# Attention's preparation rebuilt: norm scale folded into the weights' split, rows turned tile by tile, wide rotary tables; unused products during the second router's rounds

## The chip, the cores and the metric

One core of a Trainium2 chip runs one program. Its five engines each work through their own list of instructions: TensorE (PE, with its weight loads shown apart as PEld), VectorE (DVE), ScalarE (ACT), GpSimd (POOL) and SyncE (SP), which here only starts transfers. They wait for each other through semaphores. The metric is the device time of one execution in microseconds. Times inside the program are counted from the start of the profiled span.

## The reference

Two layers over 512 tokens of width 1024. Each layer mixes tokens (layer 0 by gated long convolutions, layer 1 by attention), adds a cross attention into 256 memory tokens, and then runs a mixture of 16 experts in which each expert picks its 64 best tokens. The lines that matter here:

```python
def rms_norm(x, g):
    y = xf * lax.rsqrt(jnp.mean(xf * xf, axis=-1, keepdims=True) + NORM_EPS)
    return (y * g.astype(jnp.float32)).astype(x.dtype)
...
mem_n = rms_norm(mem, mem_norm_g)
for i in range(DEPTH):
    u = rms_norm(h, mix_norm_g[i])
    if i % N_MIXERS == 0:
        proj = u @ hy_w_in[j]
        ...
    else:
        proj = u @ at_w_in[j]          # 1024 -> 768 q, 256 k, 256 v, 256 for the cross attention
        q = apply_axial_rope(rms_norm(q, at_q_norm_g[j]), cos, sin)
        kk = apply_axial_rope(rms_norm(kk, at_k_norm_g[j]), cos, sin)
        main = blocked_gqa(q, kk, vv)
    cross = memory_cross_attn(cq, mem_n, w_mem_kv[i])
    h = h + jnp.concatenate([main, cross], axis=-1) @ w_out[i]
    h = h + expert_choice_ffn(rms_norm(h, ffn_norm_g[i]), router_w[i], ...)

def expert_choice_ffn(xn, w_router, w_gate, w_up, w_down):
    aff = jax.nn.softmax((xn @ w_router).astype(jnp.float32), axis=-1)
    g, idx = lax.top_k(jnp.swapaxes(aff, 1, 2), cap)      # cap = 64
    xg = xn[bidx, idx]
    hid = silu(xg @ w_gate) * (xg @ w_up)
    y = (hid @ w_down) * g
    return jnp.zeros_like(xn).at[bidx, idx].add(y)
```

## The kernel before

By the trace the program passes through these stretches: layer 0's mixing up to about 378 us, its router up to 415, its experts up to 755, attention with its preparation up to 1016, the second router up to 1033, the second layer's experts up to 1381, and the last norm.

The residual `h` stays in SBUF as four tiles of 128 tokens by 1024. Products that need more than fp32r's precision are made of three: a number is split into a rounded high part and the rest, and `mm3` (lines 283 to 285) adds high by high, low by high and high by low. `split` (lines 230 to 240) makes the parts: ACT rounds the high one (L234 without a scale, L236 with one) and DVE, or POOL when asked, subtracts it to give the low one (L238 without, L240 with a scale). `Pair` holds both parts. `put` calls `split` on slices of a `Pair`.

A router (in `moe`, from line 937) turns the affinities onto 16 partitions by four transposes (L966), finds the 64 largest per expert in eight rounds of MAX8 and MATCH_REPLACE8 on DVE (L989, L990), turns the result back (L1000, into the bank `wb`), counts ranks (L1004, L1007), builds the one-hot matrix `oh`, and gathers the chosen rows with products (L1040) and their row factors (L1021). In layer 0 the memory's key and value products for layer 1 (`mem_kv`, L331 and L335) are issued behind the first transposes, so that PE has work beside the rounds. In layer 1 nothing stands there.

The experts' weights come through a ring of slots of 768 KB, all started by SP in one order (L524). A slot is loaded anew once the PE products that used it have run, and the first of these are the gate products L1071. The last pair's rows are added to `h` by scatter products (L1094 and L1095, pinned, that is kept in program order) and adds on DVE (L1096), eight of each; ACT takes the squares of each half tile as it is done (L1158).

Attention then loads its input weights in four blocks of 384 columns (`load_at`). DVE multiplies each by the norm's gain first (L1179, eight slices of 128 by 384 a block), then `split_at` splits it, with the low parts made in turn by POOL and DVE. The rotary tables are made on POOL (L1209, L1210, L1212) in pieces of 128 by 32. All four tiles of `h` are turned by transposes (L1228) after all scatter products, in two halves `k4` of 512 columns. Blocks are projected in the order 2 (keys and half of the values), 0, 1, 3, each tile by tile into one of two banks tagged `p`. The bank is freed by `norm_rope` (L1244 squares on ACT, L1246 to L1251 on DVE, and then L1254, L1259 on POOL and L1261 for the rotation). `head_T` (L1295 copies, L1298 transposes) starts the heads, and L1321 and L1322 are the score products.

The order on each engine is set by a scheduler that models the instructions. Only what is pinned or issued after another instruction by name is kept fixed.

Of the kernel before, what the change touches and what calls it, by code (L numbers as in the profile page):

```python
# [17 lines left out]
T = 512  # L18
# [10 lines left out]
NE = 16  # L29
# [120 lines left out]
def kernel(  # L150
# [80 lines left out]
    def split(src, hi, lo, scale=None, eng=None):  # L231
# [705 lines left out]
    def moe(layer, rt, ring):  # L937
# [61 lines left out]
        for tt in range(NT):  # L999
            PE.transpose(out=wb[:, tt * NE:(tt + 1) * NE], in_=work[:, tt * 128:(tt + 1) * 128], identity=ident[:NE, :NE])  # L1000
# [90 lines left out]
        def scatter(y, ohT, tt, n, tag):  # L1091
            sl = slice(n * 512, (n + 1) * 512)
            b = bank(tag)
            pin(PE.matmul(b, ohT.ap[:, tt * 128:(tt + 1) * 128], y.hi, start=True, stop=False))  # L1094
            pin(PE.matmul(b, ohT.ap[:, tt * 128:(tt + 1) * 128], y.lo, start=False, stop=True))  # L1095
# [6 lines left out]
        for pr in range(NE // 2):  # L1102
# [33 lines left out]
            else:  # L1136

                sq, hss = xgb.ap[:, :512], small.tile([128, 2, NT], F32, name="hsq", bufs=1)
# [14 lines left out]
            if pr == last:  # L1153
                y1 = parts(1)
                for tt in range(NT):
# [12 lines left out]
    hss = moe(0, rt, ring)  # L1168
    if stop == "moe0":
        return dump()  # L1170


    def load_at(blk):
# [3 lines left out]
        wv = fv(wb, ND, 384)  # L1177
        for k in range(ND):
            DVE.tensor_scalar(out=wv[:, k], in0=wv[:, k], scalar1=vec(MIXG + 8 + k), scalar2=None, op0=ALU.mult)  # L1179
        return wb  # L1180

    def split_at(wb, first=False):
        W = Pair(RB, ND, 384)
        for k in range(ND):
            put(W, (ALLP, k), fv(wb, ND, 384)[:, k], eng=(POOL, DVE)[[0, 1, 0, 1, 0, 1, 0, 1][k]])
# [3 lines left out]
    wb = load_at(2)  # L1189
    atpool = tc.tile_pool(name="at", bufs=1, side="right")  # L1190
    for p in RX:
        p.turn(F32R)
# [316 lines left out]
```

## Time and profile before

| what | us |
|---|---|
| median of three runs | 1397.52 (1394.19 to 1398.58) |
| the profiled execution | 1396.28 |
| its span | 1394.3 |
| PE busy | 1278.1 (92%) |
| DVE, ACT, POOL busy | 628.8 (45%), 432.9 (31%), 208.0 (15%) |
| moved by DMA over the span | 364.06 MB, mean 261 GB/s |

Busy shares are averages over stretches with different limits, so the table says little about a single stretch. A stretch is read from the windows (busy time of each engine, PE's granted clock as a share of full speed, the share of the 16 DMA engines) and from the timeline, where a bracket behind a row gives the idle time ahead of it and what ended it. An fp32 product of the program shows as two matrix instructions in the trace, a transpose as one.

### The profile page before, as it was taken

What the parts mean: (1) busy time and instruction counts of PE and PEld (TensorE: products, weight loads), DVE (VectorE), ACT (ScalarE), POOL (GpSimd) and SP (SyncE); (2) the same over time, 40 slices, a digit from 0 to 9 for tenths busy, and PEclk for the clock granted to TensorE, in tenths of its full rate; (3) what the DMA queues carried; (4) which work ended last, traced back from release to release, by engine and by line L of the source; (5) the groups of instructions that cost most, each with busy time, mean ns of one, the idle gap of its engine ahead of it and who ended that gap; (6) DMA issues with size and microseconds to landing.
All of it is one profiled execution on the core that took longest, in us unless ns stands there. A gap on an engine that the chain in (4) does not pass through costs nothing.

```text
span 1394.3 us, 17952 instructions
## 1 busy us (share of the span) xinstructions
PE 1278.1 (92%) x6986; PEld 816.9 (59%) x6986; DVE 628.8 (45%) x1239; ACT 432.9 (31%) x844; POOL 208.0 (15%) x207
## 2 busy tenths in 40 slices
PE   7998999989989999999888789999959999998985
PEld 5887878865775444444434787656744444443432
DVE  5567757777451222221214778567541222221213
ACT  6444445545221011100003458685311110110003
POOL 4342334323200000000002432021100000000001
PEclk8999999999999999999999999999969999999998
DMA  9312101315898999999998001123869999999994
GB/s 349 114 31 61 48 29 46 122 46 179 272 359 344 416 416 417 416 417 417 416 407 356 1 0 62 46 86 105 303 263 371 417 417 416 416 416 417 417 416 197
DMA packets 79046, 364.06 MB, mean 261 GB/s; under 512 B 8497, under 2 KB 17073, under 8 KB 77682
## 3 DMA queue, kind: packets, MB, share of 16 engines
q1 hardware_dynamic: 73552, 343.96, 62.7%
q0 software_dynamic: 2592, 11.54, 2.2%
q10 hardware_dynamic: 2818, 7.43, 1.4%
q8 instruction: 55, 0.90, 0.3%
q14 instruction: 29, 0.24, 0.1%
HBM read 354.51 MB, written 8.39 MB: 260 GB/s over the span
## 4 chain that ended last, share of the span: by engine, by line
PE 57%; DMA 23%; DVE 12%; ACT 3%; issue 3%; POOL 2%; SPq 0%; DVEq 0%; ACTq 0%; POOLq 0%
PE bank_e L1071 8%; PE bank_p L1071 8%; DMA farena<-in_exp_w_gate_dram 6%; DMA x<-in_exp_w_down_dram 4%; DMA x<-in_exp_w_up_dram 4%; PE bank_p L284 4%; PE bank_p L283 4%; PE bank_p L285 4%; PE bank_y L1146 4%; PE bank_e L1146 3%; PE bank_y L1342 1%; DMA farena<-p_atw_dram 1%; PE bank_m L1040 1%; DMA farena<-p_hyw_dram 1%; DMA farena<-in_exp_w_up_dram 1%
## 5 line engine op out<-in xcount | busy, mean ns | idle before, releaser
L1096 DVE TENSOR_TENSOR h<-h,bank_m 128x512 f32<-128x512 f32 x64 | 41.4, 683 | 244.8 <-PE bank_m L1095 244.8
L284 PE MATMUL bank_p<-x,x 128*128 128x512 f32 (+1 forms) x284 | 111.0, 391 | 4.0 <-POOL x L238 3.4
L285 PE MATMUL bank_p<-x,x 128*128 128x512 f32 (+1 forms) x288 | 109.6, 380 | 0.2 <-DVE x L238 0.2
L1071 PE MATMUL bank_e<-x,farena 128*64 128x384 f32 x496 | 102.8, 489 | 5.3 <-DMA x<-in_exp_w_up_dram 5.3
L1071 PE MATMUL bank_p<-farena 128*64 128x384 f32 x480 | 97.9, 490 | 8.2 <-DMA farena<-in_exp_w_gate_dram 8.2
L1025 POOL DMA_INDIRECT rows<-h_keep,rows_at x14 | 13.3, 953 | 568.3 <-DVE rows_at L1024 537.8
L240 DVE SCALAR_TENSOR_TENSOR rarena<-bank_y,gs,rarena 128x512 fp32r<-128x512 f32 x16 | 12.0, 750 | 176.1 <-ACT rarena L236 176.1
L1071 PE MATMUL bank_e<-farena 128*64 128x384 f32 x408 | 86.1, 489 | 4.8 <-DMA farena<-in_exp_w_up_dram 4.8
L1071 PE MATMUL bank_p<-x,farena 128*64 128x384 f32 x416 | 84.3, 489 | 3.9 <-DMA x<-in_exp_w_gate_dram 3.9
L283 PE MATMUL bank_p<-x,x 128*128 128x512 f32 (+1 forms) x216 | 84.3, 391 | 2.2 <-DVE h L434 1.1
L1082 ACT COPY earena<-bank_m 128x384 f32<-128x384 f32 x32 | 15.3, 479 | 227.0 <-PE bank_m L1080 227.0
L234 ACT CAST x<-farena 128x1024 fp32r<-128x1024 f32 (+2 forms) x100 | 69.3, 717 | 50.2 <-DMA farena<-p_hyw_dram 14.7
L1120 ACT ACTIVATE earena<-bank_p,gs 128x384 f32<-128x384 f32 x32 | 18.6, 581 | 194.0 <-PE bank_p L1071 194.0
L238 POOL TENSOR_TENSOR x<-farena,x 128x384 fp32r<-128x384 f32 (+2 forms) x31 | 52.5, 1705 | 174.5 <-ACT x L234 162.5
L1071 PEld LDWEIGHTS bank_e<-x,farena 128*64 128x64 f32 x496 | 42.2, 137 | 51.8 <-issue 38.7
L1071 PEld LDWEIGHTS bank_p<-farena 128*64 128x64 f32 x480 | 39.6, 137 | 52.4 <-issue 36.5
L1146 PE MATMUL bank_e<-x,earena 128*64 128x512 f32 x174 | 62.0, 596 | 3.2 <-DMA x<-in_exp_w_down_dram 3.2
L284 PEld LDWEIGHTS bank_p<-x,x 128*128 128x128 f32 x284 | 54.5, 192 | 15.8 <-POOL x L238 5.6
L1146 PE MATMUL bank_y<-x,earena 128*64 128x512 f32 x168 | 61.7, 599 | 0.9 <-DMA x<-in_exp_w_down_dram 0.7
L434 DVE TENSOR_TENSOR h<-h,bank_p 128x512 f32<-128x512 f32 x64 | 43.7, 684 | 39.0 <-PE bank_p L285 38.7
L236 ACT ACTIVATE rarena<-bank_y,gs 128x512 fp32r<-128x512 f32 x16 | 11.0, 687 | 159.1 <-PE bank_y L1146 126.2
L285 PEld LDWEIGHTS bank_p<-x,x 128*128 128x128 f32 x288 | 55.7, 193 | 7.4 <-issue 0.8
(359 smaller groups left out, 2912.5 us busy)
## 6 DMA issues: line engine op xcount, KB each, us to landing
x<-in_exp_w_up_dram SPq DMA_DIRECT2D x62, 768.0 KB, 15.0
farena<-in_exp_w_gate_dram SPq DMA_DIRECT2D x60, 768.0 KB, 15.0
farena<-in_exp_w_down_dram SPq DMA_DIRECT2D x57, 768.0 KB, 15.0
x<-in_exp_w_down_dram SPq DMA_DIRECT2D x57, 768.0 KB, 15.0
x<-in_exp_w_gate_dram SPq DMA_DIRECT2D x52, 768.0 KB, 15.0
farena<-in_exp_w_up_dram SPq DMA_DIRECT2D x51, 768.0 KB, 14.4
slot<-in_exp_w_gate_dram SPq DMA_DIRECT2D x16, 768.0 KB, 15.0
slot<-in_exp_w_up_dram SPq DMA_DIRECT2D x15, 768.0 KB, 15.0
```

Of the source, the lines that this page charges most:

```text
L234: ACT.copy(out=hi.ap if isinstance(hi, Blk) else hi[0], in_=src)
L238: return (eng or DVE).tensor_tensor(out=lo[0], in0=src, in1=hi[1], op=ALU.subtract)
L283: PE.matmul(o, L.hi[li], R.hi[ri], start=first, stop=False)
L284: PE.matmul(o, L.hi[li], R.lo[ri], start=False, stop=False)
L285: PE.matmul(o, L.lo[li], R.hi[ri], start=False, stop=last)
L434: DVE.tensor_tensor(out=h[:, tt, sl], in0=h[:, tt, sl], in1=b, op=ALU.add)
L1040: pin(PE.matmul(b[:, j * 128:(j + 1) * 128], h[:, tt, 256 * q + j:256 * (q + 1):2], ohv[:, tt], start=tt == 0, stop=tt == NT - 1))
L1071: pin(PE.matmul(banks[n][64 * e:64 * e + 64, :384], xg[:, k, 64 * e:64 * e + 64], ring.at[(nm, 2 * pr + e, q)][0][:, j, n * 384:(n + 1) * ...
L1082: ACT.copy(out=hT[n].ap, in_=b[:, :384])
L1096: DVE.tensor_tensor(out=h[:, tt, sl], in0=h[:, tt, sl], in1=b, op=ALU.add)
L1120: ACT.activation(out=hid[n].ap, in_=gb[n][:, :384], func=AF.Silu, scale=rss)
L1146: pin(PE.matmul(yb[n][64 * e:64 * e + 64], hT[g].ap[:, k * 128 + 64 * e:k * 128 + 64 * e + 64], ring.at[("d", 2 * pr + e, g, c)][0][:, i % ...
```

## The change

Five edits, all in `moe` and in attention's preparation.

1. In layer 0's router the first of four chunks of `mem_kv` is issued ahead of the affinities' transposes and is no longer bound to come after them.
2. In layer 1's router a new helper `keep_warm` issues eleven fp32 products of the identity with itself, 512 columns wide, into a bank that nobody reads; the transposes into `wb` are kept behind them.
3. Layer 0's `moe` gets `attention_begin`, which is called per tile between the last scatter products. It loads and splits block 2's weights, and turns each tile's rows once that tile is complete. The second half of the columns is split by ACT and a product with the negated identity instead of by DVE. The squares come last, into a scratch of their own in another arena.
4. `load_at` no longer scales. `split_at` folds the gain into the split: ACT's high part by L236, DVE's low part by L240, none on POOL. The weights' parts and the turned rows now lie in the ring's pieces alone.
5. The rotary tables are made four token tiles at a time, 16 products and 4 negations in place of 32 and 8.

```diff
+    def keep_warm(n):
+        b = bank("p")
+        for _ in range(n):
+            tc.keep_in_program_order(PE.matmul(b, ident, ident.unsqueeze(1).broadcast_to([128, 4, 128]), start=True, stop=True))
...
-    def moe(layer, rt, ring):
+    def moe(layer, rt, ring, then=None):
...
         if layer == 0:
+            kv = mem_kv(mTb, lambda c: mws[c], xr.rearrange("p (a b) -> p a b", a=4))
+            next(kv)
             with tc.issue_after(turned.ins):
-                drain(mem_kv(mTb, lambda c: mws[c], xr.rearrange("p (a b) -> p a b", a=4)))
+                drain(kv)
...
+        else:
+            keep_warm(11)
...
-            PE.transpose(out=wb[:, tt * NE:(tt + 1) * NE], in_=work[:, tt * 128:(tt + 1) * 128], identity=ident[:NE, :NE])
+            t = PE.transpose(out=wb[:, tt * NE:(tt + 1) * NE], in_=work[:, tt * 128:(tt + 1) * 128], identity=ident[:NE, :NE])
+            if layer:
+                tc.keep_in_program_order(t)
...
                 for tt in range(NT):
                     for n in range(2):
-                        scatter((y0, y1)[n], ohT[pr], tt, n, "me"[n])
-                        ACT.activation(out=sq, in_=h[:, tt, n * 512:(n + 1) * 512], func=AF.Square, accum_out=hss[:, n, tt:tt + 1])
+                        scatter((y0, y1)[n], ohT[pr], tt, n, "me"[n], (lambda ins: ins) if then else pin)
+                        if not then:
+                            squares(tt, n)
+                    if then and tt:
+                        then(tt - 1)
+                if then:
+                    then(NT - 1)
+                    for tt in range(NT):
+                        for n in range(2):
+                            squares(tt, n, pin)
...
-        for k in range(ND):
-            DVE.tensor_scalar(out=wv[:, k], in0=wv[:, k], scalar1=vec(MIXG + 8 + k), scalar2=None, op0=ALU.mult)
...
-            put(W, (ALLP, k), fv(wb, ND, 384)[:, k], eng=(POOL, DVE)[[0, 1, 0, 1, 0, 1, 0, 1][k]])
+            put(W, (ALLP, k), fv(wb, ND, 384)[:, k], scale=vec(MIXG + 8 + k))
...
+    def attention_begin(tt):
+        if tt == 0:
+            wb = load_at(2)
+            for p in RX:
+                p.turn(F32R)
+            at_["W2"] = split_at(wb, Arenas(*RX))
+            at_["uT"] = [Pair(Arenas(*RX), 4, T) for _ in range(2)]
+        for k4 in range(2):
+            ...
+            if k4 == 0:
+                put(uT, sl, bv)
+            else:
+                ACT.copy(out=uT.hi[sl], in_=bv)
+                PE.matmul(bv, nident, uT.hi[sl], start=False, stop=True, skip_group_check=True)
+                ACT.copy(out=uT.lo[sl], in_=bv)
...
-        for tt in range(NT):
-            for hf in range(2):
-                ...
+        for hf in range(2):
+            for tab, half, cs in ((t1, hf, 0), (t2, 1 - hf, 1)):
+                for a in range(2):
+                    POOL.tensor_tensor(out=tab[:, :, a, hf], in0=gv[:, a, half].unsqueeze(1).broadcast_to([128, NT, 16]),
+                                       in1=ropev[:, :, cs, a], op=ALU.mult)
```

A scheduler decides the order, so here is what moved at three places. In the changed kernel L470, L477, L337, L341, L972 and L1010 are what L464, L471, L331, L335, L966 and L1000 are before.

PE at the first router, before: logits (L471), affinities' transposes (L966), memory products (L331, L335), the way back (L1000).

```order
L464 MATMUL bank_m<-ident,h 128x128 x8
L471 MATMUL bank_y<-rw,farena 128x16 x8
L966 MATMUL bank_m<-ident,earena_3269 16x128 x4
L331 MATMUL bank_p<-farena 128x256 x16
L335 MATMUL bank_p<-farena 128x128 x32
L1000 MATMUL bank_m<-ident,earena_3269 128x16 x4
```

The same place in the changed kernel.

```order
L470 MATMUL bank_m<-ident,h 128x128 x4
L337 MATMUL bank_p<-farena 128x256
L470 MATMUL bank_m<-ident,h 128x128 x4
L337 MATMUL bank_p<-farena 128x256 x2
L477 MATMUL bank_y<-rw,farena 128x16 x8
L337 MATMUL bank_p<-farena 128x256 x5
L972 MATMUL bank_m<-ident,earena_3269 16x128 x4
L337 MATMUL bank_p<-farena 128x256 x8
L341 MATMUL bank_p<-farena 128x128 x32
L1010 MATMUL bank_m<-ident,earena_3269 128x16 x4
```

Eight memory products have moved ahead of the affinities' transposes: three of them ahead of the last logits, five behind these.

PE at the second router in the changed kernel, where before L1000 follows L966 directly.

```order
L477 MATMUL bank_y<-rw,farena 128x16 x8
L972 MATMUL bank_m<-ident,earena_7312 16x128 x4
L246 MATMUL bank_p<-ident 128x512 x11
L1010 MATMUL bank_m<-ident,earena_7312 128x16 x4
L1016 LDWEIGHTS earena_7312
```

The eleven unused products (L246) stand between the two transposes.

DVE at the end of the first layer's experts, before: scatter adds (L1096), the weights' scaling (L1179), low parts of the weights (`x_5004`) and of the turned rows (`x_5007`), the norm's sum (L1221).

```order
L1096 TENSOR_TENSOR h<-h,bank_m 128x512
L1096 TENSOR_TENSOR h<-h,bank_e 128x512
L1179 TENSOR_SCALAR farena<-farena,vecs 128x384 x8
L238 TENSOR_TENSOR x_5004<-farena,x_5003 128x384
L1221 TENSOR_TENSOR rs_5074<-hsq 128x4
L238 TENSOR_TENSOR x_5007<-bank_p,rarena_5012 128x4x128
```

The same place in the changed kernel, from the last add of the second tile on; `x_4969` is the weights' low part, `x_4973` that of the turned rows.

```order
L1108 TENSOR_TENSOR h<-h,bank_e 128x512
L240 SCALAR_TENSOR_TENSOR x_4969<-farena,vecs,x_4968 128x384 x8
L238 TENSOR_TENSOR x_4973<-bank_p,x_4972 128x4x128
L1108 TENSOR_TENSOR h<-h,bank_m 128x512
L1108 TENSOR_TENSOR h<-h,bank_e 128x512
L238 TENSOR_TENSOR x_4973<-bank_p,x_4972 128x4x128
L1108 TENSOR_TENSOR h<-h,bank_m 128x512
L1108 TENSOR_TENSOR h<-h,bank_e 128x512
L238 TENSOR_TENSOR x_4973<-bank_p,x_4972 128x4x128 x2
L1263 TENSOR_TENSOR rs_5106<-hsq 128x4
```

All eight low parts of block 2's weights now stand on DVE, ahead of the adds of the third and fourth tile.

## Rows read from the trace of the kernel before

**Rows 1.** Stretches: busy time and instructions of each engine, PE clock, DMA share.
```profile
core 0: us, PE busy (x) PEld busy (x) DVE busy (x) ACT busy (x) POOL busy (x), PEclk, DMA share, GB/s
412.00:424.00 12.00, 10.55 (x88) 8.66 (x88) 2.37 (x8) 0.37 (x1) 0.00 (x0) 1.00 0.76 266
...
1014.00:1032.00 18.00, 3.59 (x25) 2.89 (x25) 13.12 (x33) 2.52 (x6) 0.00 (x0) 0.52 1.00 415
1032.00:1044.00 12.00, 10.87 (x69) 9.11 (x69) 2.14 (x7) 0.00 (x0) 0.00 (x0) 0.72 0.01 4
...
1060.00:1340.00 280.00, 268.52 (x1466) 126.95 (x1462) 64.42 (x121) 27.27 (x47) 5.63 (x6) 1.00 1.02 417
```

**Rows 2.** Timeline of PE, first router: start, us, instruction, idle before and releaser.
```profile
392.34 2.48 PE L471 MATMUL bank_y<-rw,farena 128*128 128x16 f32 x16 [0.25 <-ACT farena L452]
397.47 1.01 PE L966 MATMUL bank_m<-ident,earena 128*16 128x128 f32 x4 [2.64 <-DVE earena L963]
398.27 8.14 PE L331 MATMUL bank_p<-farena 128*128 128x256 f32 x32
406.25 7.31 PE L335 MATMUL bank_p<-farena 128*128 128x128 f32 x64
413.48 0.41 PE L1000 MATMUL bank_m<-ident,earena 16*128 16x16 f32 x4
...
415.67 4.01 PE L1040 MATMUL bank_m<-oh,h 128*128 128x128 f32 x32 [1.13 <-DVE oh L993]
...
420.41 2.80 PE L1071 MATMUL bank_p<-slot,farena 128*64 128x384 f32 x16
```

**Rows 3.** Timeline of DVE, the first router's last round.
```profile
409.77 0.66 DVE L990 MATCH_REPLACE8 earena<-m,earena 16x512 f32<-16x512 f32 x1
```

**Rows 4.** Timeline of PE, second router.
```profile
1017.91 1.01 PE L966 MATMUL bank_m<-ident,earena 128*16 128x128 f32 x4 [2.00 <-DVE earena L963]
1031.02 0.58 PE L1000 MATMUL bank_m<-ident,earena 16*128 16x16 f32 x4 [12.09 <-DVE earena L990]
...
1033.40 6.39 PE L1040 MATMUL bank_m<-oh,h 128*128 128x128 f32 x32 [1.13 <-DVE oh L993]
...
1040.52 2.80 PE L1071 MATMUL bank_p<-x,farena 128*64 128x384 f32 x16
```

**Rows 5.** Timeline of PE, attention's preparation: three waits and the first score product.
```profile
766.85 0.41 PE L283 MATMUL bank_p<-x,rarena 128*128 128x384 f32 x1 [2.76 <-DVE x L238]
...
772.09 0.69 PE L284 MATMUL bank_p<-x,rarena 128*128 128x384 f32 x1 [3.78 <-POOL x L238]
...
817.68 1.11 PE L1298 MATMUL bank_m<-ident,farena 128*128 128x128 f32 x4 [3.37 <-DVE x L238]
...
827.87 0.50 PE L1321 MATMUL bank_e<-x,x 128*128 128x512 f32 x1
```

**Rows 6.** Groups by line, 745 to 1015: count, busy us, mean ns, idle before, releasers.
```profile
L283 PE MATMUL bank_p<-x,rarena 128*128 128x384 f32 (+1 forms) x72 | 26.7, 373 | 7.7 <-ACT farena L1278 3.3 <-DVE x L238 2.8 <-DVE farena L1251 1.3
```

**Rows 7.** POOL's groups, shapes apart, 745 to 1015.
```profile
L238 POOL TENSOR_TENSOR x<-farena,x 128x384 fp32r<-128x384 f32 x16 | 18.1, 1142 | 29.3 <-ACT x L234 26.1 <-PE bank_m L1333 2.4 <-PE bank_p L285 0.8
```

**Rows 8.** Timeline of DVE: scaling of block 2, and one rotation product twice.
```profile
762.06 3.45 DVE L1179 TENSOR_SCALAR farena<-farena,vecs 128x384 f32<-128x384 f32 x8
...
807.20 0.56 DVE L1254 TENSOR_TENSOR farena<-farena 128x384 f32<-128x384 f32 x1
...
812.66 0.96 DVE L1254 TENSOR_TENSOR farena<-farena 128x384 f32<-128x384 f32 x1
```

**Rows 9.** Timeline of ACT: a square, and six high parts of block 2's weights.
```profile
757.97 0.64 ACT L1158 ACTIVATE farena<-h 128x512 f32<-128x512 f32 x1 [1.47 <-DVE h L1096]
...
765.33 2.57 ACT L234 CAST x<-farena 128x384 fp32r<-128x384 f32 x6
```

**Rows 10.** The page's costliest groups: a low part with a scale.
```profile
L240 DVE SCALAR_TENSOR_TENSOR rarena<-bank_y,gs,rarena 128x512 fp32r<-128x512 f32 x16 | 12.0, 750 | 176.1 <-ACT rarena L236 176.1
```

**Rows 11.** A stretch after the heads start, columns as in the first group.
```profile
840.00:860.00 20.00, 19.21 (x99) 12.96 (x97) 19.14 (x43) 19.63 (x41) 7.08 (x8) 1.00 0.23 80
```

More of the change, by code (lines that the diff above doesn't have):

```diff
@@ L1136, in moe @@
             else:
-                sq, hss = xgb.ap[:, :512], small.tile([128, 2, NT], F32, name="hsq", bufs=1)
+                hss = small.tile([128, 2, NT], F32, name="hsq", bufs=1)
                 tc.keep_in_program_order(ACT.activation(out=hss[:, 0, 0:1], in_=eps_t, func=AF.Sqrt))
@@ L1154, in moe, with squares @@
                 y1 = parts(1)
+                sqb = EA.alloc(256)
+                def squares(tt, n, keep=lambda ins: ins):
+                    keep(ACT.activation(out=sqb.ap.bitcast(BF16), in_=h[:, tt, n * 512:(n + 1) * 512], func=AF.Square, accum_out=hss[:, n, tt:tt + 1]))
                 for tt in range(NT):
                     for n in range(2):
-                        scatter((y0, y1)[n], ohT[pr], tt, n, "me"[n])
-                        ACT.activation(out=sq, in_=h[:, tt, n * 512:(n + 1) * 512], func=AF.Square, accum_out=hss[:, n, tt:tt + 1])
+                        scatter((y0, y1)[n], ohT[pr], tt, n, "me"[n], (lambda ins: ins) if then else pin)
[8 more added lines that the diff above has]
+                            squares(tt, n, pin)
+                sqb.free()
                 y0.free()
@@ L1176, in load_at, with split_at @@
         SP.dma_start(out=wb.ap, in_=p_atw[blk])
-        wv = fv(wb, ND, 384)
+        return wb
+    def split_at(wb, arena):
+        W = Pair(arena, ND, 384)
         for k in range(ND):
-            DVE.tensor_scalar(out=wv[:, k], in0=wv[:, k], scalar1=vec(MIXG + 8 + k), scalar2=None, op0=ALU.mult)
-        return wb
-    def split_at(wb, first=False):
-        W = Pair(RB, ND, 384)
-        for k in range(ND):
-            put(W, (ALLP, k), fv(wb, ND, 384)[:, k], eng=(POOL, DVE)[[0, 1, 0, 1, 0, 1, 0, 1][k]])
+            put(W, (ALLP, k), fv(wb, ND, 384)[:, k], scale=vec(MIXG + 8 + k))
         wb.free()
         return W
-    wb = load_at(2)
+    at_ = {}
+    def attention_begin(tt):
[6 more added lines that the diff above has]
+        for k4 in range(2):
+            uT, sl = at_["uT"][k4], (ALLP, ALLP, slice(tt * 128, tt * 128 + 128))
+            b = bank("py"[k4] if tt % 2 else "p")
+            for kk in range(4):
+                k = 4 * k4 + kk
+                PE.matmul(b[:, kk * 128:(kk + 1) * 128], h[:, tt, k * 128:(k + 1) * 128], ident, is_transpose=True, start=kk == 0, stop=kk == 3)
+            bv = b.rearrange("p (a c) -> p a c", a=4)
+            if k4 == 0:
[4 more added lines that the diff above has]
+                ACT.copy(out=uT.lo[sl], in_=bv)
+    hss = moe(0, rt, ring, attention_begin)
+    if stop == "moe0":
+        return dump()
+    W2, uT = at_["W2"], at_["uT"]
     atpool = tc.tile_pool(name="at", bufs=1, side="right")
-    for p in RX:
-        p.turn(F32R)
     RB = Arenas(*RX, Arena(atpool.__enter__().tile([128, RB_SIZE], F32R, name="rarena2"), RB_SIZE))
@@ L1215 @@
     router_w(1)
-    W2 = split_at(wb, True)
-    uT = [Pair(RB, 4, T) for _ in range(2)]
     rs1 = small.tile([128, 4], F32, name="rs1", bufs=1)
@@ L1222 @@
     rstd(rs1, D)
-    for k4 in range(2):
-        for tt in range(NT):
-            b = bank("ppeemmye"[4 * k4 + tt])
-            for kk in range(4):
-                k = 4 * k4 + kk
-                PE.transpose(out=b[:, kk * 128:(kk + 1) * 128], in_=h[:, tt, k * 128:(k + 1) * 128], identity=ident)
-            put(uT[k4], (ALLP, ALLP, slice(tt * 128, tt * 128 + 128)), b.rearrange("p (a c) -> p a c", a=4))
     qkpool = tc.tile_pool(name="qk", bufs=1)
@@ L1265, in project_at @@
     def project_at(blk, W=None):
[L1266 removed]
+        W = W or split_at(load_at(blk), RB)
         for tt in range(NT):
```

20 lines of the change are left out of this document (6 added, 14 removed).

## The prediction

> **What bounds the kernel now.** I read the stretches first [rows 1]. In the expert stretches the transfers set the end: from 1060 to 1340 the DMA share is 1.02, at 417 GB/s. PE looks busy there (268.52 of 280 us) but serves the transfers. Such a stretch ends when its last weights have arrived, and these flow again only once PE's first gate products (L1071) free slots. So what a router saves ahead of its first L1071 should arrive at the end one for one, as long as the stream stands still meanwhile: at the second router the share is 0.01 from 1032 to 1044, with every slot full. Between the two expert stretches there is no stream to wait for, and PE's waits count.
>
> Then PE's timeline at three places: both routers and attention's preparation.
>
> First router [rows 2, 3]: DVE's last round ends at 409.77 + 0.66 = 410.43, but PE only comes to L1000 at 413.48, since 32 memory products (L331) and 64 (L335) stand ahead of it. PE is 3.05 us late. Before that it idles 2.64 us for the softmax.
>
> Second router [rows 4]: here PE waits 12.09 us for the rounds, and the following gather (L1040, L1021) runs on a slow clock: 1033.40 to the first L1071 at 1040.52 are 7.12 us, where the first router needs 420.41 - 415.67 = 4.74 for the same. The granted clock is 0.52 and 0.72 in these windows, against 1.00 at the first router's gather [rows 1]; half of full speed is the lower of the two levels (1.2 and 2.4 GHz).
>
> Attention's preparation [rows 5, 6]: between the last scatter product and the first score product at 827.87, PE waits 2.76 us for the first low parts of the weights, 3.78 for POOL's low part of one slice, some 4.6 for banks that ACT and DVE free (L1278 and L1251 in the grouped row), and 3.37 for DVE ahead of the first head.
>
> **First router's memory products.** Sixteen trace products of L331 (eight of the program) leave the place behind L966. One costs (406.25 - 398.27)/32 = 0.249 us, so PE's queue shortens by 4.0 us, more than the 3.05 it is late. Five of the eight run in the 2.64 us of idle and cost nothing as long as that wait lasts. The other three stand ahead of the last logits and delay these by up to 6 x 0.249 = 1.5 us, less the idle of 0.25 there and what they find free between the transposes. I take a delay of 0.9. Gain 3.05 - 0.9 = 2.1 us; bounds: 3.05 if nothing is delayed, and 1.0 if the delay is whole and pushes the five behind the softmax by another half microsecond.
>
> **Second router's unused products.** Their bank and PE are free, so the price is only that L1000 stands behind them. One shows as two in the trace, and has 512 columns where L331 has 256, so it costs 4 x 0.249 = 1.0 us with the same start from a cold clock: eleven take 11.0 us and end at 1018.92 + 11.0 = 1029.9, just ahead of the rounds (1031.02). If the clock holds, the gather takes 4.74 for 7.12 (-2.38) and L1000 0.41 for 0.58, together -2.55. Between the products' end and the gather lie the sparse 2.4 us from 1031.02 to 1033.40 and about one more, in which the clock may fall again. I take -2.0. Bounds: -2.55, and +5.5 if the clock never rises. For that end I take the cold gather's 6.39/32 = 0.20 us for 128 columns, eight times that for a product, 17.6 for eleven, so L1000 at 1036.5. The nearest row is against this end: the products of L331 run from a cold start too and average 0.249, not 0.40.
>
> **Attention's preparation, the start.** DVE loses the scaling: 8 x 0.43 = 3.45 us for block 2 [rows 8], and as much for each of three more. It gains four low parts a block that POOL made before (18.1 us of POOL's time [rows 7]), and each of its eight becomes L240. The trace has that with 512 columns at 0.75 us [rows 10], which is 0.56 for 384. DVE's sum per block stays near 4.5 us. What changes is the place: the eight stand ahead of the adds of the third and fourth tile. Today the eight adds end as the scaling starts, 762.06, some 0.6 apart, so the first tile is complete near 758.5; transposes and rounding of its first half take 0.8. ACT's eight high parts follow at 2.57/6 = 0.43 each [rows 9], from about 759.3 on. DVE follows from 759.8 to 764.2; two tiles' low parts and four adds of some 0.65 end near 768.2, and after the last transposes the first projection product starts about 769.4, for 766.85 today. It is late by 2.5, but nothing behind it waits on POOL: the 3.78 go, and the slow clock after them. What is late next is the squares. They stand behind all casts on ACT, eight of 0.64, which I take as 0.76 with an accumulator read each, 6.1 us. The norm's factor comes near 777.8 and the first bank is free around 781, so the third tile starts at about 781.1 for 782.22: gain 1.1. Bounds: 4 (the bank is free as soon as the two tiles are done) and -2.
>
> A DVE instruction of two SBUF inputs costs more beside POOL: L1254 took 0.56 us alone and 0.96 beside it [rows 8]. The tables no longer wait for the squares' scratch and may fall into the eight low parts. Eight times 0.40 are 3.2 us, the other bound; the tables' 20 instructions cover only part of them, and I take 1.0 of loss.
>
> The Trainium skill ("SBUF — State Buffer", section "Who interferes with whom") says that such a DVE instruction contends with a GpSimd instruction that reads SBUF, and that whoever comes first holds the shared port pair for its whole length. The two times of L1254 agree. By the rule alone, with a table product ahead of each of the eight, the whole 3.2 would be lost here, and the sum below would be 7.2 and not 9.4.
>
> **Attention's preparation, the rest.** The bank waits of some 3.6 behind the first (of the 4.6) and DVE's share in them shrink: no scaling between a tile's reductions, and no POOL beside the rotation (0.40 apiece, by the same two rows). Against this, the next block's parts go to the same two pieces that PE still reads, slice by slice behind its last products. Placing the rows of the order with these durations gives the second block's first tile about 4.5 us earlier than today and the first score product at 820.6, 7.3 earlier, with the 3.37 before it still there. From it I take 1.0 for a cold stretch of clock and the 1.0 for POOL: gain 5.3. Bounds: 1 and 10. Four waits sum to 2.76 + 3.78 + 4.6 + 3.37 = 14.5, and that a third stays is certain. Wide tables save only POOL time, which is not waited for after this.
>
> **Sum.** 2.1 + 2.0 + 5.3 = 9.4 us off the profiled execution's 1396.28, which lies 1.24 under the median 1397.52. I apply it to the median: 1388.1, say 1388.
>
> **The rivals.** *The preparation's gain is given back.* After the heads start ACT is busy 19.63 and DVE 19.14 of 20 us in 840 to 860 [rows 11], so what comes earlier may only queue there. PE is at 19.21 too, which speaks against it. What stays of the 5.3 is perhaps 1: 1397.5 - 5.1 = 1392.4.
>
> *The unused products bring nothing.* The clock has fallen by the gather: 1390.1. Against it, PE's idle time shrinks from 12.09 to about one microsecond.
>
> *The single pair of pieces serializes the blocks (slower).* If a block's eight high parts wait for the last product that reads the piece, and not slice by slice, each of three block changes costs 8 x 0.43 + 0.56 + 0.5 = 4.5 us of idle PE, and of the preparation only the 1.1 stays: 1397.5 - 5.2 + 13.5 = 1405.8. It decides from 3.1 us a change on. Against it, the order lists the parts one by one with waits of their own; for it, before had a spare piece.
>
> *More than expected.* The first bank is not waited for and the third wait vanishes: 4.5 more, about 1383.
>
> *The change does less than it says*, with the memory products ahead of the transposes delaying the softmax by all they save: 2.1 less, 1390, inside the range.
>
> **How the numbers follow.** Forecast 0.50 with its own range 1384.5 to 1391.5; given back 0.18 (half of it within 0.3%); unused products without effect 0.13; serialized 0.07; more 0.12. A measurement of this kernel can tell about 0.3% from no change, 4.2 us, so faster means below 1393.3 and slower above 1401.7. Faster: 0.50 + 0.09 + 0.13 + 0.12, less 0.01 for tails = 0.83; same 0.10; slower 0.07. The range leaves out the serialized case and the outer part of "more": 1381.5 to 1394.
>
> **What would show it.** First router: L1010 starts within half a microsecond of the last round, and L1052's gather about 2 us earlier. Second: eleven L246 end before the last MATCH_REPLACE8, the granted clock is 1.00 from there on, and gather to first L1083 takes under 5.2 us. Preparation: no wait on POOL, first score product at 818 to 824 less what the router saved, and the same lead at the second router. Wrong would be: idle of 4 us at each block change, L246 still running when the rounds end, or a second expert stretch that begins earlier and ends no earlier.

## The result and the profile after

The changed kernel takes 1388.01 us (median of 5 runs, 1384.48 to 1388.51) against 1396.96 before (5 runs of the same sitting). The ratio is 0.9931, 95% interval 0.9912 to 0.9949: faster by about 0.7%, at the 1388 that was forecast. The profiled execution's span went from 1394.3 to 1386.3, and PE's rows divide the 8.0 us between them so:

| from, to (rows of PE), us | before | after | difference |
|---|---|---|---|
| start, last projection product of layer 0 (unchanged code) | 389.99 | 391.51 | +1.5 |
| to the first gate product (L1071, now L1083) | 30.42 | 27.08 | -3.3 |
| to the first scatter product of the last pair | 335.29 | 335.77 | +0.5 |
| to the first score product | 72.17 | 64.06 | -8.1 |
| to the second router's affinity transposes | 190.05 | 192.78 | +2.7 |
| to the second first gate product | 22.60 | 21.53 | -1.1 |
| to the end | 353.8 | 353.6 | -0.2 |

PE's timeline at the first router of the changed kernel (start, duration, instruction, idle time before) answers to [rows 2, 3].

```profile
396.45 2.40 PE L337 MATMUL bank_p<-farena 128*128 128x256 f32 x10
398.99 0.60 PE L972 MATMUL bank_m<-ident,earena 128*16 128x128 f32 x4
...
402.88 7.31 PE L341 MATMUL bank_p<-farena 128*128 128x128 f32 x64
411.69 0.39 PE L1010 MATMUL bank_m<-ident,earena 16*128 16x16 f32 x4 [1.50 <-DVE earena L1000]
...
413.85 4.01 PE L1052 MATMUL bank_m<-oh,h 128*128 128x128 f32 x32 [1.13 <-DVE oh L1003]
...
418.59 2.80 PE L1083 MATMUL bank_p<-slot,farena 128*64 128x384 f32 x16
```

L1010 now waits 1.50 us for the rounds where L1000 was 3.05 late, and the idle gap ahead of the transposes is filled: L972 has no bracket and takes 0.60 where L966 took 1.01. The next rows are the second router's, for [rows 4].

```profile
1011.19 1.01 PE L972 MATMUL bank_m<-ident,earena 128*16 128x128 f32 x4 [1.94 <-DVE earena L969]
1012.00 11.72 PE L246 MATMUL bank_p<-ident 128*128 128x512 f32 x22
1024.30 0.39 PE L1010 MATMUL bank_m<-ident,earena 16*128 16x16 f32 x4 [0.58 <-DVE earena L1000]
...
1026.46 5.53 PE L1052 MATMUL bank_m<-oh,h 128*128 128x128 f32 x32 [1.14 <-DVE oh L1003]
...
1032.73 2.80 PE L1083 MATMUL bank_p<-x,farena 128*64 128x384 f32 x16
```

The eleven products (22 in the trace) end in time, but the gather behind them still takes 5.53 us. The windows show the clock there. In them the columns are the stretch and its length, busy time (count) of PE, PEld, DVE, ACT and POOL, PE's granted clock, the DMA share and GB/s.

```profile
392.00:400.00 8.00, 7.87 (x54) 6.97 (x54) 3.19 (x11) 5.22 (x9) 0.00 (x0) 1.00 1.02 421
764.00:772.00 8.00, 6.78 (x26) 5.70 (x27) 3.94 (x7) 4.36 (x8) 0.00 (x0) 0.50 0.00 0
...
900.00:907.00 7.00, 7.00 (x18) 3.45 (x18) 3.50 (x8) 3.23 (x8) 2.35 (x1) 0.51 0.02 5
1017.00:1024.00 7.00, 6.72 (x16) 2.66 (x14) 6.69 (x15) 0.00 (x0) 0.00 (x0) 1.00 1.01 422
1027.00:1029.00 2.00, 2.00 (x11) 2.00 (x11) 0.00 (x0) 0.00 (x0) 0.00 (x0) 0.50 0.01 3
```

The clock is 1.00 (the 2.4 GHz level) in the second half of the unused products (1017 to 1024), and 0.50 (1.2 GHz) in the gather: it fell after the 2.7 us between them, in which PE ran little. It is also low at attention's start (764 to 772) and once more at 900 to 907, amid attention. At the first router, 392 to 400, it is 1.00; before, the same window has 0.60 and PE busy for 5.11 us in place of 7.87:

```profile
392.00:400.00 8.00, 5.11 (x26) 4.36 (x26) 3.63 (x12) 4.54 (x8) 0.00 (x0) 0.60 1.03 424
```

Next, attention's start, first block 2's low parts on DVE.

```profile
758.74 4.32 DVE L240 SCALAR_TENSOR_TENSOR x<-farena,vecs,x 128x384 fp32r<-128x384 f32 x8 [0.26 <-issue]
```

POOL at the same time has this.

```profile
739.81 0.87 POOL L1254 TENSOR_TENSOR farena<-farena 128x64 f32<-128x64 f32 x3
740.65 0.70 POOL L1257 TENSOR_SCALAR farena<-farena 128x64 f32<-128x64 f32 x2
781.29 1.17 POOL L1294 TENSOR_TENSOR farena<-farena 128x128 f32<-128x128 f32 x2 [39.94 <-DVE farena L1286]
```

And PE has these three rows among others.

```profile
762.71 0.50 PE L1230 MATMUL bank_p<-x,nident 128*128 128x512 f32 x1 [2.75 <-ACT x L1229]
...
770.39 0.67 PE L289 MATMUL bank_p<-x,x 128*128 128x384 f32 x1
...
781.69 0.44 PE L289 MATMUL bank_p<-x,x 128*128 128x384 f32 x1 [0.85 <-ACT farena L1313]
```

Eight low parts take 4.32 us, one every 0.54, with POOL idle: the tables were done at 741, not beside them. The first projection product starts at 770.39 and the third tile at 781.69. PE's waits from 755 to 1016 (us in total, times, longest) answer to [rows 5, 6]:

```profile
PE bank_p L1230 <- ACT x L1229: 3.4, 2, 2.7
...
PE bank_m L1333 <- DVE rarena L238: 1.1, 1, 1.1
PE bank_p L289 <- ACT farena L1313: 0.9, 1, 0.9
```

The waits on POOL (3.8) and on the first low parts (2.8) are gone. The one ahead of the first head (L1333 is what L1298 was) is down from 3.4 to 1.1, and of the bank waits of 4.6 some 1.4 are left (0.9 here and 0.5 in a smaller row). What is new is a wait of 3.4 for ACT's parts of the turned rows.

With the wait ahead of the first head a stretch of low clock went too. Before, it lies right behind that wait:

```profile
817.00:823.60 6.60, 5.92 (x21) 5.83 (x22) 4.41 (x10) 1.20 (x3) 1.15 (x2) 0.50 0.00 0
```

The kernels without the fold (before, e3, e5 below) have it in their profiled executions, and none of those with the fold has it.

### The profile page after: what moved, and what is told of

Its sections match the earlier page's. It is cut to its first block, busy times and chain, and to the rows that moved or that the text cites. A ratio compares the mean times of both kernels' runs of the same rounds, so it can differ in the third digit from the quotient of the medians.

```text
span 1386.3 us, 17944 instructions
## 1 busy us (share of the span) xinstructions
PE 1291.6 (93%) x7012; PEld 823.3 (59%) x7012; DVE 613.0 (44%) x1219; ACT 439.4 (32%) x848; POOL 186.0 (13%) x171
## 5 line engine op out<-in xcount | busy, mean ns | idle before, releaser
L290 PE MATMUL bank_p<-x,x 128*128 128x512 f32 (+1 forms) x348 | 132.5, 381 | 3.7 <-POOL x L238 3.3
L289 PE MATMUL bank_p<-x,x 128*128 128x512 f32 (+1 forms) x288 | 109.4, 382 | 4.2 <-ACT x L234 1.4
L291 PE MATMUL bank_p<-x,x 128*128 128x512 f32 (+1 forms) x288 | 108.0, 375 | 0.2 <-DVE x L238 0.2
L1083 PE MATMUL bank_p<-farena 128*64 128x384 f32 x504 | 101.0, 489 | 7.1 <-DMA farena<-in_exp_w_gate_dram 7.1
L1083 PE MATMUL bank_e<-x,farena 128*64 128x384 f32 x504 | 101.9, 488 | 3.8 <-DMA x<-in_exp_w_up_dram 3.8
L240 DVE SCALAR_TENSOR_TENSOR rarena<-bank_y,gs,rarena 128x512 fp32r<-128x512 f32 x16 | 12.0, 751 | 178.2 <-ACT rarena L236 178.2
L1083 PE MATMUL bank_e<-farena 128*64 128x384 f32 x392 | 85.3, 489 | 4.0 <-DMA farena<-in_exp_w_up_dram 4.0
L1083 PE MATMUL bank_p<-x,farena 128*64 128x384 f32 x392 | 82.0, 490 | 4.8 <-DMA x<-in_exp_w_gate_dram 4.8
L1132 ACT ACTIVATE earena<-bank_p,gs 128x384 f32<-128x384 f32 x32 | 18.6, 581 | 192.9 <-PE bank_p L1083 192.9
L290 PEld LDWEIGHTS bank_p<-x,x 128*128 128x128 f32 x348 | 66.4, 191 | 15.3 <-POOL x L238 4.0
L1083 PEld LDWEIGHTS bank_p<-farena 128*64 128x64 f32 x504 | 42.1, 137 | 51.9 <-issue 37.7
L234 ACT CAST x<-farena 128x512 fp32r<-128x512 f32 (+1 forms) x70 | 56.5, 815 | 51.2 <-DMA farena<-p_hyw_dram 16.3
L1083 PEld LDWEIGHTS bank_e<-x,farena 128*64 128x64 f32 x504 | 42.4, 137 | 50.8 <-issue 40.1
L1158 PE MATMUL bank_e<-x,earena 128*64 128x512 f32 x180 | 67.3, 596 | 4.0 <-DMA x<-in_exp_w_down_dram 4.0
L1158 PE MATMUL bank_y<-x,earena 128*64 128x512 f32 x174 | 64.4, 599 | 2.1 <-DMA x<-in_exp_w_down_dram 2.0
L289 PEld LDWEIGHTS bank_p<-x,x 128*128 128x128 f32 x288 | 54.8, 191 | 15.4 <-DVE h L440 2.8
L236 ACT ACTIVATE rarena<-bank_y,gs 128x512 fp32r<-128x512 f32 x16 | 11.0, 687 | 161.1 <-PE bank_y L1158 127.7
L238 POOL TENSOR_TENSOR x<-farena,x 128x1024 fp32r<-128x1024 f32 (+1 forms) x17 | 39.3, 2323 | 157.6 <-ACT x L234 148.7
```

The costliest lines, as they stand in the source:

```text
L234: ACT.copy(out=hi.ap if isinstance(hi, Blk) else hi[0], in_=src)
L289: PE.matmul(o, L.hi[li], R.hi[ri], start=first, stop=False)
L290: PE.matmul(o, L.hi[li], R.lo[ri], start=False, stop=False)
L291: PE.matmul(o, L.lo[li], R.hi[ri], start=False, stop=last)
L1083: pin(PE.matmul(banks[n][64 * e:64 * e + 64, :384], xg[:, k, 64 * e:64 * e + 64], ring.at[(nm, 2 * pr + e, q)][0][:, j, n * 384:(n + 1) * ...
L1132: ACT.activation(out=hid[n].ap, in_=gb[n][:, :384], func=AF.Silu, scale=rss)
```

## The experiments

The table has the median, the ratio to the kernel before in the same sitting, and four distances of the profiled execution: G1, from the last projection product of layer 0 to the first gate product; S, from the first scatter product of the last pair to the first score product; A, from there to the second router's transposes; G2, from these to the first gate product.

| kernel | median us | ratio, 95% interval | G1 | S | A | G2 |
|---|---|---|---|---|---|---|
| before | 1396.96 | | 30.42 | 72.17 | 190.05 | 22.60 |
| after | 1388.01 | 0.9931 (0.9912 to 0.9949) | 27.08 | 64.06 | 192.78 | 21.53 |
| e1_no_warm | 1388.97 | 0.9942 (0.9915 to 0.9969) | 29.46 | 61.96 | 195.85 | 21.85 |
| e2_no_early_kv | 1392.28 | 0.9972 (0.9953 to 0.9990) | 30.44 | 63.46 | 190.08 | 21.54 |
| e3_old_attention | 1394.85 | 0.9989 (0.9973 to 1.0004) | 27.08 | 71.95 | 190.13 | 22.44 |
| e4_warm_gather | 1386.31 | 0.9928 (0.9903 to 0.9953) | 29.49 | 62.24 | 189.81 | 20.01 |
| e5_scale_apart | 1395.20 | 0.9987 (0.9969 to 1.0006) | 29.46 | 73.65 | 189.55 | 20.86 |
| e6_narrow_tables | 1388.54 | 0.9943 (0.9923 to 0.9962) | 27.08 | 63.97 | 189.86 | 22.74 |
| e8_adds_first | 1389.59 | 0.9944 (0.9923 to 0.9966) | 29.54 | 62.35 | 190.10 | 22.59 |
| e9_warm_both | 1382.09 | 0.9906 (0.9881 to 0.9932) | 27.02 | 63.95 | 189.71 | 20.01 |
| e10_all | 1387.38 | 0.9916 (0.9886 to 0.9946) | 27.01 | 63.40 | 195.85 | 20.02 |
| e11_squares_free | 1381.31 | 0.9883 (0.9851 to 0.9914) | 27.02 | 59.91 | 191.19 | 20.01 |
| e12_fold_alone | 1386.85 | 0.9927 (0.9899 to 0.9956) | 30.49 | 61.14 | 191.49 | 21.62 |
| e13_fold_and_warm | 1382.91 | 0.9887 (0.9869 to 0.9905) | 27.02 | 60.54 | 191.82 | 21.21 |

Executions of one kernel lie several microseconds apart (1390.41 to 1404.31 for 25 runs of before in one sitting), so edits of 1 or 2 us are read from the distances and not from the medians. A distance is that of one execution, and the clock moves it too: with the tile by tile turning and the fold unchanged, S is 61.96 in e1, where no stretch of it has the low clock, and 64.06 in the changed kernel, where some 10 us of it have.

**e1_no_warm**, the changed kernel without the call:

```diff
-        else:
-            keep_warm(11)
```

> The changed kernel without the eleven unused products. Theory (the products raise the clock for the rounds' second half, but it falls again in the sparse microseconds ahead of the gather, so they are worth the 1.07 us by which the second router shortened from L972 to the first L1083): that distance goes back from 21.5 to 22.6 us, the gather L1052 from 5.5 to 6.4, and the time from 1388.0 to about 1389.1. Rival (the forecast's 2.0): the distance grows to 23.5 and the time to 1390. Rival (worth nothing, the difference between the traces comes from elsewhere): the distance stays at 21.5.

Measured: G2 is 21.85, 0.3 more than in the changed kernel, and the median 1.0 more. The gather (from its start to the first gate product) took 6.36 us without the products and 6.26 with them. In three other kernels that have them (e3, e6, e8) the gather took 7.13, 7.47 and 7.32 us and G2 was 22.4 to 22.7, as before. Over all kernels of the table, G2 is 21.95 as a mean of the six with just these products (after, e2, e3, e5, e6, e8) and 22.02 as a mean of the three without them (before, e1, e12). So no gain of theirs is shown, and the rival that they bring nothing fits better than the forecast's 2.0.

**e2_no_early_kv**, all memory products behind the transposes again:

```diff
-            kv = mem_kv(mTb, lambda c: mws[c], xr.rearrange("p (a b) -> p a b", a=4))
-            next(kv)
             with tc.issue_after(turned.ins):
-                drain(kv)
+                drain(mem_kv(mTb, lambda c: mws[c], xr.rearrange("p (a b) -> p a b", a=4)))
```

> The changed kernel with all memory products behind the affinities' transposes again. Theory (the early chunk is worth 1.8 us at the first router, and the stream of weights hands it on to the end of the first expert stretch): the first L1083 moves from 418.6 back to about 420.4, the first scatter product from 754.4 to about 755.8, the time from 1388.0 to 1389.5. Rival (the stream absorbs it): the first L1083 moves back but the first scatter product stays within 0.4 us of 754.4 and the time within 0.5 of 1388.

Measured: G1 returns to 30.44, 3.36 more. From the first gate product to the first scatter product it took 334.86 us here and between 334.8 and 336.9 in all fourteen kernels, whatever G1 was. So the stream hands the gain on, and the chunk is worth 3.4 us where the gather is fast. The median is 4.3 above that of the changed kernel; the profiled execution, at 1385.80, was the fastest of twelve, and what kept the others slower has not been seen.

**e3_old_attention**, the kernel before with the two router edits alone (as in the change's first two hunks).

> The kernel before with the two router edits alone (early memory chunk, eleven unused products); attention's preparation as before. Theory (5.4 us of the 8 come from the preparation): from the first scatter product to the second router's transposes it takes 262.2 us as before, against 256.8 in the changed kernel, and the time is 1397 less about 2.6, 1394.0. Rival (the preparation's lead is an effect of an earlier start): below 259 us and below 1391.

Measured: S is 71.95, as before, and the time can't be told from before. The preparation's lead is its own, as the theory has it.

**e4_warm_gather**, one unused product more, behind the rank counts, which are kept in program order for it (that part of the edit is not shown):

```diff
+        if layer:
+            keep_warm(1)
```

> The changed kernel with one more unused product between the rank counts and the second router's gather, where PE idles 1.1 us. Theory (the clock falls because of the sparse 2.7 us between the last unused product and the gather): the granted clock stays 1.00 through the gather, L1052's 32 products take 4.0 us and not 5.5, the first L1083 comes 1.4 us earlier, the time falls to about 1386.6. Rival (the fall has another cause, or the product delays the gather): the gather still takes over 5 us, the time stays at 1388 or rises by up to 0.9.

Measured, on PE at the second router:

```profile
1019.50 0.39 PE L1010 MATMUL bank_m<-ident,earena 16*128 16x16 f32 x4 [0.96 <-DVE earena L1000]
...
1020.38 1.10 PE L246 MATMUL bank_p<-ident 128*128 128x512 f32 x2
1021.66 4.01 PE L1055 MATMUL bank_m<-oh,h 128*128 128x128 f32 x32 [0.17 <-DVE oh L1003]
```

The product fills the gap of 1.1 us, the gather takes 4.01, and G2 falls to 20.01. The same 4.74 us from gather to gate product came out in all four kernels that have this product in this place with the tile by tile turning (e4, e9, e10, e11), against 6.01 to 7.47 in the six that have the eleven alone. So the gap with little work is what the clock fell on. Filling it did not hold the clock each time: in e13 below, with the same product in the same place, the clock was low again and it took 5.55. Why is open, and whether the one product would do without the eleven was not run.

**e5_scale_apart**, the gain multiplied by DVE first and the low parts shared with POOL, all else as changed:

```diff
+        for k in range(ND):
+            DVE.tensor_scalar(out=wv[:, k], in0=wv[:, k], scalar1=vec(MIXG + 8 + k), scalar2=None, op0=ALU.mult)
...
-            put(W, (ALLP, k), fv(wb, ND, 384)[:, k], scale=vec(MIXG + 8 + k))
+            put(W, (ALLP, k), fv(wb, ND, 384)[:, k], eng=(POOL, DVE)[k % 2])
```

> The changed kernel with the norm's gain multiplied into the weights by DVE first, as before, and the low parts made in turn by POOL and DVE; the tile by tile turning and all else stay. Theory (folding the scale is what shortens the preparation: 3.45 us of DVE per block ahead of the split, and POOL beside the rotation): from the first scatter product to the first score product it takes about 68 us, against 62 to 64 with the fold and 72 before. Rival (the gain comes from turning the tiles early): 63 to 65 us. The time 1392 or 1388.

Measured: S is 73.65, above before's 72.17, and the time can't be told from before. The wait ahead of the first head (L1336) is back among PE's waits (total, times, longest), and so is the low clock behind it; L1227 are the transposes that turn the tiles:

```profile
PE bank_p L1227 <- ACT x L1234: 4.3, 1, 4.3
PE bank_m L1336 <- DVE rarena L238: 3.4, 1, 3.4
```

So the theory held, and further than it went: without the fold nothing of the gain is left. What is called the fold here is one edit with two effects, in e5 as in e12: DVE no longer multiplies ahead of the split, and POOL no longer makes half of the low parts. Neither was run by itself.

**e12_fold_alone**, the kernel before with the fold and nothing else (the same two hunks the other way).

> The kernel before with one edit only: the norm's gain folded into the weights' split, all low parts on DVE; rows turned after all scatter products, narrow tables, the routers as before. Theory (the fold is the greater part of the preparation's 8 to 10 us, turning tile by tile the smaller): 65 to 67 us from the first scatter product to the first score product against 72.2 before and 62 to 64 in the changed kernel; the median 1391 to 1393. Rival (the fold needs the early turning, since without it the parts wait for ACT): 70 us or more, the median within 1.5 of before. Other rival (the fold is all of it): 62 to 64 us.

Measured: S is 61.14, and the ratio 0.9927 is as good as the whole change's 0.9931. The other rival is right: the fold is all of the preparation's gain, and turning the rows tile by tile adds nothing that shows. From the first scatter product to the second router's transposes (S and A together) it takes 252.6 us here and 252.1 to 253.8 in e2, e4, e6, e8 and e9, which turn tile by tile. PE waits longer at the start than before (2.76 in [rows 5]) and yet hardly at all behind it, by its timeline:

```profile
767.43 0.69 PE L283 MATMUL bank_p<-x,rarena 128*128 128x384 f32 x1 [4.40 <-DVE x L238]
...
796.09 0.41 PE L283 MATMUL bank_p<-x,rarena 128*128 128x384 f32 x1 [0.31 <-DVE farena L1248]
```

**e6_narrow_tables**, the tables in pieces of 128 by 32 as before.

> The changed kernel with the rotary tables in pieces of 128 by 32 as before, 32 products and 8 negations. Theory (the tables now end at 741, before POOL or DVE are wanted, so their width is worth nothing): all tables still end before 760, no wait on POOL, the time stays at 1388 within 1.5. Rival (the width keeps them out of the split's way): table products run beside DVE's low parts after 758 and the first score product comes 1 to 3 us later.

Measured: the last table instruction starts at 741.39, S is 63.97, the median within 0.6. The width is worth nothing that shows. Before, half of the tables started only at 765, and the profile names ACT's squares (L1158), whose scratch lies in the same arena, as what they waited for. That wait went with the third edit, and in e12, which leaves the squares as they were, it is still there (765.57, after 24.41 us of idle).

**e8_adds_first**, block 2's weights split behind the last scatter add:

```diff
+        if add:
+            with tc.issue_after(add.ins):
+                for k in range(ND):
+                    put(at_["W2"], (ALLP, k), fv(at_["wb"], ND, 384)[:, k], scale=vec(MIXG + 8 + k))
```

> The changed kernel with block 2's weights split only after the last scatter add, so that the turned rows' parts and the adds of the third and fourth tile no longer stand behind eight parts. Theory (the 2.75 us wait on ACT at 762.7 and the late adds come from that order): no such wait, the last transposes end near 765, the first projection product starts about 766 instead of 770.4, and the first score product comes 3 to 4 us earlier (59 to 60 us behind the first scatter product for 62 to 64). Rival (the parts are then late themselves, and the squares behind them on ACT still free the first bank at the same time): the first projection product is earlier by under 1.5 us or starts and stalls, and the distance stays at 62 to 64.

Measured on PE:

```profile
764.88 0.44 PE L289 MATMUL bank_p<-x,x 128*128 128x384 f32 x1 [0.24 <-ACT x L1236]
778.08 0.51 PE L289 MATMUL bank_p<-x,x 128*128 128x384 f32 x1 [4.35 <-ACT farena L1318]
```

The first projection product came 5 us earlier, and 4.35 of that returned as a wait for the first bank, behind the squares. S is 62.35. The rival is right in what it names.

**e9_warm_both**: the product of e4 in both routers (with the rank counts and the transposes ahead of them kept in program order), and one more behind the first router's memory products.

```diff
                 drain(kv)
+                keep_warm(1)
...
+        keep_warm(1)
```

> The changed kernel with an unused product between the rank counts and the gather of both routers, and one more behind the first router's memory products, where PE now idles 1.5 us. Theory (the clock falls in some executions at the first router's gather too, as it took 7.1 us and not 4.7 in two of four runs with the early chunk; the products hold it): both gathers take 4.7 to 4.9 us, the first L1083 comes 27 us behind the last projection product in every run, the median falls to about 1385.5. Rival (the products delay L1010 or the gather): the distance is above 27.5 us, the median above 1387.

Measured: both gathers took 4.74 us, G1 is 27.02, the median 1382.09 and below that expected.

**e10_all** (e8 and e9 together) and **e11_squares_free**, which also takes the squares out of their fixed place behind ACT's casts:

```diff
-                        if not then:
-                            squares(tt, n)
+                        squares(tt, n)
...
-                    for tt in range(NT):
-                        for n in range(2):
-                            squares(tt, n, pin)
```

> Both routers' gathers kept on the fast clock, and block 2's weights split after the last scatter add. Theory (the order of the split is worth about 1.2 us, since the first bank then waits for the squares): 62.3 us from the first scatter product to the first score product, both gathers 4.74, the median 1382 less 1, about 1381. Rival (nothing left): 1382 or above.

> The same with the squares issued tile by tile with the adds, no longer behind all of ACT's casts. Theory (the 4.35 us stall at the third tile came from the squares and the norm's factor behind them): the third tile starts without a wait over 1 us, and the first score product comes 58 to 60 us behind the first scatter product, the median about 1379.5. Rival (ACT is full at this place, so that squares ahead delay the parts instead): the first projection product comes 3 to 5 us later, distance 62 to 65, median 1382 or above.

Measured: e10's S is 63.40 with the wait of 4.3 still there, and its median is above that expected; its profiled execution lost 6 us in A, with the clock low in two stretches there. In e11 that wait is gone, S is 59.91 and the median 1381.31: the squares were what held the bank.

**e13_fold_and_warm**: before, with the fold, the early chunk, the eleven products and e9's, rows turned as before.

> The kernel before with the fold, the early memory chunk and the products that keep both gathers on the fast clock; rows still turned after all scatter products, narrow tables. Theory (the fold alone carries the preparation's gain, and turning tile by tile adds nothing): 61 to 62 us from the first scatter product to the first score product, both gathers 4.74, the median 1386.9 less 3.3 and 2.6, about 1381 within 2. Rival (turning tile by tile is needed beside an earlier start): 64 us or more, the median 1384 or above.

Measured: S is 60.54 and the median 1382.91. Of the gathers only the first took 4.74. At the second the product itself ran slow (1.86 us, where e4's took 1.10):

```profile
1018.98 1.86 PE L246 MATMUL bank_p<-ident 128*128 128x512 f32 x2
1020.63 4.82 PE L1054 MATMUL bank_m<-oh,h 128*128 128x128 f32 x32
```

e11 and e13 are the fastest of the study, at 0.9883 (0.9851 to 0.9914) and 0.9887 (0.9869 to 0.9905), and can't be told apart. e13's interval lies wholly below the changed kernel's, so this version beats both, by 5.1 us of the medians over the changed kernel; e11's touches it.

## Why the prediction was right, point by point

**First router: 2.1 forecast, 3.3 found.** That PE would be on time and DVE bound was right, and so was the passing on. The term that was mis-sized is the delay of 0.9 for the three products ahead of the last logits. It did not come: from the last projection product to the transposes it takes 7.48 us before and 7.49 after. With the gap filled, PE's clock is 1.00 from 392 to 400, where it was 0.60 before, and the logits and transposes run faster by what the new products cost. What the text did not see is the other side. L1010 now waits 1.5 us, and the gather behind it fell to the slow clock in four of seven kernels with the chunk but without e9's products (e1, e4, e5, e8: G1 of 29.5). There the gain is 0.9. As a mean of the seven it is 2.0, so the forecast's 2.1 is near the mean by luck, and the 3.3 is one of two outcomes.

**Second router: 2.0 forecast, 1.1 found in the profiled execution, and nothing by the means of G2 with and without the products (21.95 and 22.02).** Price and end of the products were right (11.7 us for 11.0, done before the rounds). The failed step is that the clock would mostly hold from the products' end to the gather. It does not. The rival had the mechanism, and e4 showed what helps in four kernels of five.

**Preparation: 5.3 forecast, 8.1 found to the first score product and 5.4 to the second router.** The total agrees by luck, for the inner steps failed. The start was to gain 1.1: the third tile begins 27.33 us behind the first scatter product and began 26.52 behind it before, so the start lost 0.8. Its first projection product comes 4.9 us later than before, where 2.5 were counted; the new wait on ACT's casts and the slow clock lie there. "That a third stays is certain" was wrong: of the four waits' 14.5 us some 2.5 are left, 1.4 for banks and 1.1 ahead of the first head. Behind the start 8.9 us were gained where 6.2 were counted. The waits for banks make some 3 of them and the wait ahead of the head 2.3. Most of the rest is what the low clock of 817 to 823.6 cost before, some 3 us by estimate: half of PE's 5.92 busy us there. The text had kept the 3.37 and does not name that clock. The 1.0 for POOL beside the low parts was not due, since the tables ended at 741. The 1.0 for a slow clock was due. And 2.7 us went again behind the heads' start: e2 has the same code there and up to 900 the same busy times, but not the slow clock. The windows of the changed kernel:

```profile
890.00:900.00 10.00, 8.95 (x42) 5.39 (x41) 5.90 (x18) 7.28 (x19) 0.00 (x0) 1.00 0.18 50
900.00:910.00 10.00, 10.00 (x32) 5.30 (x31) 4.55 (x12) 5.54 (x16) 2.35 (x1) 0.66 0.21 56
```

And those of e2:

```profile
890.00:900.00 10.00, 8.95 (x42) 5.39 (x41) 5.91 (x18) 7.25 (x19) 0.00 (x0) 1.00 0.17 52
900.00:910.00 10.00, 9.48 (x44) 5.42 (x42) 7.55 (x19) 8.57 (x23) 3.83 (x2) 1.00 0.20 55
```

So "given back by busy ACT and DVE" is not what happened: A is 189.5 to 190.1 in all kernels without a slow stretch there, with the fold (e2, e4, e6, e8, e9) and without it (before, e3, e5); after, e1, e10, e11, e12 and e13 have one and more.

The reason for the gain was in the text (no scaling between a tile's reductions, no POOL beside the rotation), and e5 and e12 show that these two together carry it; the early turning, on which the forecast of the start rests, adds nothing that shows. One sum of the text is wrong here: that DVE's work per block "stays near 4.5 us". It does not stay but falls. Over the four blocks, 745 to 1015, it was this before (busy us, mean ns):

```profile
L1179 DVE TENSOR_SCALAR farena<-farena,vecs 128x384 f32<-128x384 f32 x32 | 16.5, 552 | 0.3 <-DMA farena<-p_atw_dram 0.3
L238 DVE TENSOR_TENSOR x<-farena,x 128x384 fp32r<-128x384 f32 x16 | 11.3, 712 | 0.0
```

And in the changed kernel:

```profile
L240 DVE SCALAR_TENSOR_TENSOR x<-farena,vecs,x 128x384 fp32r<-128x384 f32 x32 | 18.6, 616 | 0.5 <-issue 0.3 <-ACT x L236 0.2
```

So DVE went from 27.8 us to 18.6 for the same parts, and POOL's 18.1 [rows 7] are gone.

**The slower rival** (one pair of pieces serializes the blocks) is excluded: behind the start no wait of PE up to the first head is above 1.1 us. **The rule on the shared port** (the Trainium skill, "SBUF — State Buffer", "Who interferes with whom") did not decide here, since POOL stood idle beside block 2's low parts. The text's two times of L1254 are not "alone" and "beside": the 0.56 began at 807.20 and POOL's rotation at 807.31, the 0.96 began at 812.66 behind POOL's at 812.35. That the slow one is the one that came second agrees with the rule. So does the changed kernel: an L240 that began at 790.41, with POOL's rotation running since 789.77, took 0.82 us, where the one before it, begun ahead of POOL at 789.55, and each of block 2's eight, with POOL idle, took 0.61.

## What to carry to other kernels

Ask of a combined edit which single part carries it, by doing that part alone: here one multiplication folded into an instruction that ran anyway, with POOL's share of the parts given to DVE, was worth as much as the whole rebuilding. An engine that makes what PE needs next is read by its own list of instructions, not by its busy share. Where products are put in to hold the clock, look at the last microseconds ahead of the work that they are for: eleven products that ended 2.7 us ahead of it did not show a gain, and one in the gap did in four kernels of five.

## What the runs showed of the hardware that was not expected

The same instructions in the same order ran at either clock in different kernels' executions. The first router's gather, with one fixed order of products ahead of it, took 4.74 us to the first gate product in the changed kernel, e3 and e6, and 7.07 to 7.19 in e1, e4, e5 and e8. Attention behind the heads' start took 190 us, or 191 to 196 with the clock low in stretches of it. PE has gaps ahead of the gather. Filling them with products made the gather 4.74 in every profiled execution with it at the first router (e9, e10, e11, e13). It was 4.74 without the early chunk too (before, e2, e12).
